# Softmax weights left undivided through the products with v, with one over the sum multiplied in at the silu gate

## The chip, the cores and the metric

The kernel runs on one core of a Trainium2 chip. TensorE (PE) does the matmuls and the transposes, VectorE (DVE) and GpSimd (POOL) the elementwise work, ScalarE (ACT) the activations, and SyncE (SP) issues the DMA transfers from one queue in order. The metric is device microseconds of one execution. Before the change the median of 3 runs is 1141.21 us (1140.96 to 1142.23).

## The reference

One encoder layer with two gated attention branches runs in float32 on a prompt of 512 tokens and a sample of 1024, with shared weights:

```python
h = rmsnorm(x, norm_g)
qa, ka, va, za, qb, kb, vb, zb, ga, gb = split(h @ w_in)
# branch A: 8 heads, 8 x 16 neighbourhood on a grid; branch B: 8 heads on 2 kv heads, window 128, one sink logit per head
s = q @ k.T / 8 + bias
p = softmax(s)                 # in branch B over [s, sink], the sink's own weight dropped
oa = (p @ va) * silu(za) @ w_o_a
ob = (p @ vb) * silu(zb) @ w_o_b
y = x + (sigmoid(ga) * oa + sigmoid(gb) * ob) @ w_out
```

The softmax's division stands ahead of the product with v; as one over the sum is the same for all keys of a query, it may as well stand behind it.

## The kernel before, in words

Every float32 operand is kept as two halves, a rounded one (names ending in hi, hh, fh) and the remainder (lo, hl, fl), and a product is three matmuls: rounded by rounded, rounded by remainder, remainder by rounded (L761 for the projections, L1286 to L1288 for the dense products). The program does the prompt first and then the sample, each in two phases.

The **attention phase** walks six groups of heads, A0 to A3 with two heads each and B0 and B1 with four. A group loads its weights `w` (L600), has them split by ACT (L602) and DVE or POOL (L607), projects 128 tokens at a time (L761), normalises q and k (DVE L785, POOL L792 and L799, DVE L816), and transposes them on PE (L861). `attend` (L908) computes a block's scores (PE L934). `weigh` (L958) then adds the bias on DVE while keeping the running extreme `mx` (L969), and takes the exponential on ACT with its sum `sm` as a by-product (L978). For branch B it adds the sink to the sum by three small operations (POOL L994, ACT L997, POOL L999). It takes one over the sum (DVE L1002), multiplies each 128 x 256 or 128 x 384 tile of weights `sb` by it (DVE L1010 or POOL L1008), transposes the weights on PE (L1026), splits them (ACT L1032, DVE L1037), multiplies by v on PE (L1063), and stores the outputs to `o_d` in DRAM.

The **dense phase** first computes the gate inputs z, chunk by chunk (c = 0 to 7, 128 channels each, 512 tokens at a time). `post_z` (L1406) takes the silu on ACT (L1395), loads the attention outputs back as `ot` (L1417), for chunks 4 to 7 adds two of them, and multiplies them into the gate (helper `tt`, L1162, on DVE or POOL). Its result is needed only when the merge products start, after the gates g. Weight tiles `raw` are loaded (L1250), split (L1168, L1173) and used by PE, in part by Strassen's scheme. Some gate products, called fills, are pulled ahead into the attention phase (`fill_gates`, L1474, its raw weights in two `fr` buffers, bank `d`).

What sets the order: the operations are recorded with a priority, engines they may run on and a planned time, and a list scheduler (`Flow.run`, L207) replays them against those planned times; an operation goes into an engine's queue when it is planned to be ready, the lowest priority number first. The queues so written are fixed and each engine works its own in order. So an edit of one operation can move all others. The planner multiplies planned times of ACT, DVE and POOL by `SLACK` 1.1 in the attention phase.

The z products beyond the first two wait for `exps_done` (L1133), which follows all exponentials, since the silu needs another table on ACT.

Of the kernel before, what the change touches and what calls it, by code (L numbers as in the profile page):

```python
# [40 lines left out]
P = 128  # L41
# [313 lines left out]
def encoder_kernel(  # L355
# [45 lines left out]
        rpb_x[geo.nt] = dpool.tile([8, P, 3 * geo.cw * 16], F32, tag=f"rpb_x{geo.nt}", name=f"rpb_x{geo.nt}")  # L401
    r_d = dpool.tile([NT_S // P, P], F32, tag="r_d", name="r_d")
    t_d = dpool.tile([4, 4, P, NT_S // 2], F32, tag="t_d", name="t_d")
    o_d = {geo.nt: dpool.tile([2, 8, P, geo.nt], F32, tag=f"o_d{geo.nt}", name=f"o_d{geo.nt}") for geo in (gp, gs)}

    def expand(geo, h, lo):
# [24 lines left out]
    def bank(tag):  # L431
        return f.value(pspool, [P, 512], F32, tag, BANKS[tag])
# [215 lines left out]
    def attention_phase(geo, hh, hl, h_ops, mask_d, early, late):  # L648

        nb, nt = geo.nb, geo.nt  # L650
        kt = f.value(early, [P, 4, nt], F32R, "kt", 1)
        stores = {(c, n): [] for c in range(8) for n in range(nt // 512)}
        exps = []

        def tile_(shape, dt, tag, bufs):
            return f.value(early if tag in ("sq", "ss", "rs_v", "rs_r", "v", "q", "qt", "qk") else late, shape, dt, tag, bufs)
# [248 lines left out]
            )  # L905
            return q, [a, b]

        def attend(br, gi, g, batch, nb_t, info, prio):  # L908

            nh = 2 if br == "A" else 4  # L910
            k0 = 2 * (gi % 2)
            states = []
            for block in batch:
                sums = tuple(tile_([P, 4], F32, tag, 3) for tag in ("mx", "sm", "rs", "es"))
                pss = [bank("x") for _ in range(nh)]
                sbs = [tile_([P, GW], F32, "sb", 8 if nt == NT_S else 9) for _ in range(nh)]
                states.append((block, sums, pss, sbs))

            def places(block):
                runs, tiles, _ = block  # L920
                return runs, tiles, len(tiles) * P, tiles[1] - tiles[0], br == "A" and shifted

            def emit(e):

                for block, _, pss, _ in states:
# [18 lines left out]
            o = f.op(  # L944
                (("pe", ns),), emit, prio, new=[v for _, _, pss, sbs in states for v in (*pss, *sbs)],
                use=[queries(block) for block in batch], after=[o for b in batch for t in b[1] for o in info[t][2]],
                hold=[kt],
            )
            for block, _, _, sbs in states:
                for sb in sbs:  # L950
                    sb.writers.clear()
                for s in (k0, k0 + 1):
                    for t in block[1]:
                        reads.setdefault((s, t), []).append(o)
            for state in states:
                weigh(br, gi, g, *state, nb_t, info, prio)

        def weigh(br, gi, g, block, sums, pss, sbs, nb_t, info, prio):  # L958

            nh = 2 if br == "A" else 4  # L960
            runs, tiles, table = block
            nw = len(tiles)
            width = nw * P
            mx, sm, rs, es = sums

            def score(i, ps, sb):
                def emit(e, i=i, ps=ps, sb=sb):
                    init = 3.0e38 if br == "A" else nsink[:, 4 * g + i : 4 * g + i + 1]
                    dve.tensor_tensor_reduce(  # L969
                        out=sb.t[:, :width], in0=ps.t[:, :width], in1=bias_of(br, nb_t, i, table), scale=1.0,  # L970
                        scalar=init, op0=ALU.add, op1=ALU.min, accum_out=mx.t[:, i : i + 1],
                    )

                kw = {"new": [mx], "into": [sb]} if i == 0 else {"into": [mx, sb]}
                d = f.op((("dve", DVE_(width) + 60),), emit, prio, use=[ps, nb_t, sink_v], **kw)

                def emit(e, i=i, sb=sb):
                    act.activation(  # L978
                        sb.t[:, :width], sb.t[:, :width], AF.Exp, bias=mx.t[:, i : i + 1], scale=-1.0,
                        accum_out=sm.t[:, i : i + 1],  # L980
                    )

                kw = {"new": [sm], "into": [sb]} if i == 0 else {"into": [sm, sb]}
                x = f.op((("act", ACT_(width) + 182),), emit, prio, use=[sb], after=[d], **kw)
                exps.append(x)
                mx.left += 1
                x.vals = [*x.vals, mx]

            for i, (ps, sb) in enumerate(zip(pss, sbs)):
                score(i, ps, sb)  # L990
            if br == "B":
                f.op(
                    (("pool", 160),),
                    lambda e: nc.gpsimd.tensor_tensor(es.t, mx.t, nsink[:, 4 * g : 4 * g + 4], op=ALU.subtract),  # L994
                    prio, new=[es], use=[mx],
                )
                f.op((("act", 100),), lambda e: act.activation(es.t, es.t, AF.Exp), prio, use=[es], into=[es])  # L997
                f.op(
                    (("pool", 160),), lambda e: nc.gpsimd.tensor_tensor(sm.t, sm.t, es.t, op=ALU.add),  # L999
                    prio, use=[es, sm], into=[sm],  # L1000
                )
            f.op((("dve", 90),), lambda e: dve.reciprocal(rs.t[:, :nh], sm.t[:, :nh]), prio, new=[rs], use=[sm])  # L1002
            for i in range(nh):

                def emit(e, i=i):
                    sb = sbs[i].t[:, :width]
                    if e == "pool":
                        nc.gpsimd.tensor_tensor(sb, sb, rs.t[:, i : i + 1].to_broadcast([P, width]), op=ALU.mult)  # L1008
                    else:
                        dve.tensor_scalar(sb, sb, rs.t[:, i : i + 1], None, op0=ALU.mult)  # L1010

                f.op(
                    (("dve", 68 + 0.68 * width), ("pool", 30 + 2 * width)), emit, prio,
                    use=[rs, sbs[i]], into=[sbs[i]],
                )
            blocks = [(c, i) for c in range(nw) for i in range(nh)]
            pts = []
            for b in range(0, len(blocks), 4):
# [75 lines left out]
            else:  # L1094
                for e in range(2):
# [6 lines left out]
                    for c in (4 + 2 * g, 5 + 2 * g):  # L1102
                        for n in range(nt // 512):
                            stores[c, n].append(o)

        f.slack = SLACK
        groups = [("A", 0), ("A", 1), ("A", 2), ("A", 3), ("B", 0), ("B", 1)]
        for gi, (br, g) in enumerate(groups):
# [10 lines left out]
                for i in range(4)  # L1119
            ]  # L1120
            nb_t = tables(br, g, lead - 1)
            info, waiting = {}, []
            for t in range(nb):
                prio = lead + t
                v, qk = project(br, w, t, prio)
                info[t] = (v, *make_qk(br, gi, t, qk, prio))
                waiting += [b for b in (a_blocks if br == "A" else b_blocks) if max(b[1]) == t]
                size = 2 if br == "A" else 1
                while len(waiting) >= size:
                    batch, waiting = waiting[:size], waiting[size:]  # L1130
                    attend(br, gi, g, batch, nb_t, info, prio - (bool(waiting) or t < nb - 1))
        f.slack = 1
        exps_done = f.op((("act", 0),), lambda e: None, prio, after=exps)  # L1133
        return stores, exps_done, exps[-40]

    def dense_phase(geo, hh, hl, h_ops, o_stores, exps_done, start, opened, tp, up, p0, p1, p2, x_t, y_t, classic, fill, after_gates=None, side=None):
# [269 lines left out]
        def post_z(c, a, n, v, in_psum, prio):  # L1406
# [13 lines left out]
            ot, ov, sv = ots[0], lambda: ots[0].t[:, :n], lambda: sg.t[:, :n]  # L1420
            if len(ots) > 1:
                tt(ov, ov, lambda: ots[1].t[:, :n], ALU.add, n, prio, use=ots, into=[ot])
            if c < 4:
# [363 lines left out]
```

## Time and profile before

| | |
|---|---|
| median of 3 runs | 1141.21 us |
| profiled execution: its time, its span | 1145.24 us, 1143.4 us |
| PE busy | 1129.6 us of the span, 6115 matmuls |
| DVE, ACT, POOL busy | 858.3, 645.1, 319.4 us |
| granted PE clock, mean | 0.998 |
| prompt attention, prompt dense, sample attention, sample dense | about 0 to 214, 214 to 397, 397 to 788, 788 to 1143 us |

The span runs from the first to the last instruction; what is outside it in the profiled execution is 1.84 us. A row of a group gives line, engine, operation, tiles, shape and count, then busy us, mean ns of one, and the idle time of the engine just before with what ended it. Matmul durations overlap: the time PE needs for one is seen from one start to the next.

### The profile page before, as it was taken

The numbers are of one execution on the slowest core, as the hardware profiler recorded it, in microseconds if no ns is written. First come the engines' busy times: TensorE is split into PE (matmuls) and PEld (weight loads), VectorE is DVE, ScalarE is ACT, GpSimd is POOL, SyncE is SP. The second block draws the span as 40 slices with busy tenths as digits, with TensorE's granted clock in tenths as the row PEclk, the third lists the DMA queues.
The fourth block names the chain that finished last, engine by engine and source line by source line (L and its number), as shares of the span: only waits on it lengthen the run. The fifth ranks groups of instructions, "written<-read, shape, count | busy, mean of one in ns | idle before, by whom it ended". The sixth has DMA issues, their size and how long they took to land.

```text
span 1143.4 us, 18577 instructions
## 1 busy us (share of the span) xinstructions
PE 1129.6 (99%) x6115; PEld 981.9 (86%) x6115; DVE 858.3 (75%) x1994; ACT 645.1 (56%) x1477; POOL 319.4 (28%) x420
## 2 busy tenths in 40 slices
PE   8999999999999999999999999999999999999998
PEld 7989988888888889999899988888888888788887
DVE  6868797587766467887868888886878665497984
ACT  6767997544433246574659888875633334342320
POOL 4644443000010044443514343420123221032110
PEclk9999999999999999999999999999999999999999
DMA  7844643488797422121313214135767545564072
GB/s 267 275 140 129 189 118 97 106 257 256 237 277 210 157 91 72 29 79 29 91 31 93 72 38 121 46 111 160 262 179 228 194 161 186 196 230 130 28 221 93
DMA packets 129314, 168.26 MB, mean 147 GB/s; under 512 B 28809, under 2 KB 67473, under 8 KB 129218
## 3 DMA queue, kind: packets, MB, share of 16 engines
q1 hardware_dynamic: 129218, 167.08, 47.9%
q8 instruction: 48, 0.79, 0.3%
q14 instruction: 48, 0.39, 0.1%
HBM read 128.22 MB, written 43.54 MB: 150 GB/s over the span
## 4 chain that ended last, share of the span: by engine, by line
PE 92%; DMA 3%; DVE 2%; ACT 1%; POOL 1%; issue 1%; SPq 0%; POOLq 0%; DVEq 0%; ACTq 0%
PE p L761 23%; PE x L1288 10%; PE x L1287 10%; PE x L1286 10%; PE x L1063 5%; PE x L1026 5%; PE x L934 5%; PE p L1287 4%; PE p L1286 4%; PE p L1288 4%; PE d L1286 4%; PE d L1288 4%; PE d L1287 4%; PE x L861 2%; DMA w<-in_w_att_dram 1%
## 5 line engine op out<-in xcount | busy, mean ns | idle before, releaser
L761 PE MATMUL p<-whi,hh 128*128 128x384 f32 x384 | 133.8, 349 | 0.0
L761 PE MATMUL p<-whi,hl 128*128 128x384 f32 x384 | 132.7, 345 | 0.0
L761 PE MATMUL p<-wlo,hh 128*128 128x384 f32 x384 | 132.3, 345 | 0.0
L978 ACT ACTIVATE sb<-sb,mx 128x384 f32<-128x384 f32 (+1 forms) x192 | 107.8, 566 | 24.1 <-DVE mx L969 23.7
L761 PE MATMUL p<-whi,hb 128*128 128x384 f32 x384 | 107.8, 346 | 0.0
L1168 ACT ACTIVATE whi<-raw 128x512 fp32r<-128x512 f32 (+1 forms) x124 | 73.8, 607 | 60.2 <-PE x L1287 29.5
L1287 PE MATMUL x<-T,whi 128*128 128x512 f32 x256 | 99.7, 390 | 0.2 <-DVE T L1173 0.2
L1286 PE MATMUL x<-T,whi 128*128 128x512 f32 x256 | 99.7, 389 | 0.0
L1288 PE MATMUL x<-T,wlo 128*128 128x512 f32 x256 | 99.6, 389 | 0.0
L1037 DVE TENSOR_TENSOR pp<-x,pp 128x512 fp32r<-128x512 f32 (+1 forms) x136 | 82.6, 638 | 20.8 <-ACT pp L1032 19.7
L1288 PE MATMUL x<-hh,wlo 128*128 128x512 f32 (+1 forms) x232 | 89.8, 387 | 0.0
L1287 PE MATMUL x<-hl,whi 128*128 128x512 f32 (+1 forms) x232 | 89.8, 387 | 0.0
L1286 PE MATMUL x<-hh,whi 128*128 128x512 f32 (+1 forms) x232 | 89.8, 387 | 0.0
L1173 POOL TENSOR_TENSOR wlo<-raw,whi 128x512 fp32r<-128x512 f32 (+1 forms) x27 | 35.6, 1323 | 182.7 <-ACT whi L1168 182.6
L1173 DVE TENSOR_TENSOR wlo<-raw,whi 128x512 fp32r<-128x512 f32 (+1 forms) x97 | 65.3, 680 | 25.8 <-ACT whi L1168 25.4
L1032 ACT ACTIVATE pp<-x 128x512 fp32r<-128x512 f32 (+1 forms) x136 | 71.0, 560 | 24.0 <-PE x L1026 22.8
L799 POOL TENSOR_TENSOR rs_r<-rs_v,mhalf 128x4 f32<-128x4 f32 (+1 forms) x72 | 79.6, 1106 | 5.7
L792 POOL TENSOR_SCALAR rs_v<-ss 128x4 f32<-128x4 f32 (+1 forms) x72 | 26.8, 373 | 182.3 <-DVE ss L785 179.6
L1063 PE MATMUL x<-pp,v 128*128 128x256 f32 (+1 forms) x368 | 76.7, 322 | 0.0
L761 PEld LDWEIGHTS p<-whi,hl 128*128 128x128 f32 x384 | 73.1, 190 | 1.3 <-issue 1.0
L761 PEld LDWEIGHTS p<-whi,hh 128*128 128x128 f32 x384 | 73.1, 190 | 1.1 <-issue 0.5
L761 PEld LDWEIGHTS p<-wlo,hh 128*128 128x128 f32 x384 | 73.0, 190 | 0.9 <-issue 0.5
(351 smaller groups left out, 3012.9 us busy)
## 6 DMA issues: line engine op xcount, KB each, us to landing
raw<-in_w_g_dram SPq DMA_DIRECT2D x84, 256.0 KB
w<-in_w_att_dram SPq DMA_DIRECT2D x46, 384.0 KB
ot<-o_d SPq DMA_DIRECT2D x36, 256.0 KB
g_d<-C SPq DMA_DIRECT2D x34, 256.0 KB
raw<-in_w_z_dram SPq DMA_DIRECT2D x32, 256.0 KB
raw<-in_w_out_dram SPq DMA_DIRECT2D x32, 256.0 KB
fr<-in_w_g_dram SPq DMA_DIRECT2D x28, 256.0 KB
C<-g_d SPq DMA_DIRECT2D x24, 256.0 KB
```

Source lines behind the costliest of these rows:

```text
L761: pe.matmul(ps.t[:, :GW], part[u](k), mv.t[:, c], start=k == 0 and m == 0, stop=k == KC - 1 and m == 2,)
L799: lambda e: nc.gpsimd.tensor_tensor(r.t[:, :nn], rv.t[:, :nn], mhalf[:, :nn], op=ALU.pow),
L934: pe.matmul(pss[2 * pair + i].t[:, :width], q.t[rows, u, at : at + P], kv[:, tiles[0] : tiles[-1] + 1 : step], start=n == 0, stop=n == 2,)
L978: act.activation(sb.t[:, :width], sb.t[:, :width], AF.Exp, bias=mx.t[:, i : i + 1], scale=-1.0, accum_out=sm.t[:, i : i + 1],)
L1032: lambda e, pt=pt, pp=pp, nn=nn: act.activation(pp.t[:, 0, :nn], pt.t[:, :nn], AF.Copy),
L1037: lambda e, pt=pt, pp=pp, nn=nn: dve.tensor_tensor(pp.t[:, 1, :nn], pt.t[:, :nn], pp.t[:, 0, :nn].bitcast(F32), op=ALU.subtract),
L1063: pe.matmul(out(), v.t[:, vs], mv(), start=first, stop=last)
L1168: (("act", ACT_(n)),), lambda e: act.activation(hi(), src(), AF.Copy), prio,
L1173: lambda e: engines[e].tensor_tensor(lo(), src(), hi().bitcast(F32), op=ALU.subtract), prio,
L1286: pe.matmul(out, hi.t[:, cs], mh(), start=first and k == 0, stop=False, **more)
L1287: pe.matmul(out, hi.t[:, cs], ml(), start=False, stop=False, **more)
L1288: pe.matmul(out, lo.t[:, cs], mh(), start=False, stop=last and k == len(ws) - 1, **more)
```

## The change

The multiplication of the weights by one over the sum is taken out of `weigh`, with the reciprocal and the three sink operations of each block. `mx` and `sm` are now one tile each per group, with a column for each head and block. After a group's last block a new function `norms` does the sink operations and the reciprocal once on the whole tile, transposes it on PE, copies it on ACT and stores it to a DRAM tensor `n_d` (one row per head). `post_z` loads the two heads' rows of its chunk, each spread over 64 partitions, into an `fr` buffer `rn`, and multiplies `ot` by it before the gate. `exps_done` also waits for the sink exponentials of `norms`.

```diff
@@ attention_phase, weigh
-            mx, sm, rs, es = sums
+            mx, sm = sums
+            col = lambda i: slice(i * nb + c0, i * nb + c0 + 1)
+            c0 = (a_blocks if br == "A" else b_blocks).index(block)
...
-            if br == "B":
-                f.op(
-                    (("pool", 160),),
-                    lambda e: nc.gpsimd.tensor_tensor(es.t, mx.t, nsink[:, 4 * g : 4 * g + 4], op=ALU.subtract),
-                    prio, new=[es], use=[mx],
-                )
-                f.op((("act", 100),), lambda e: act.activation(es.t, es.t, AF.Exp), prio, use=[es], into=[es])
-                f.op(
-                    (("pool", 160),), lambda e: nc.gpsimd.tensor_tensor(sm.t, sm.t, es.t, op=ALU.add),
-                    prio, use=[es, sm], into=[sm],
-                )
-            f.op((("dve", 90),), lambda e: dve.reciprocal(rs.t[:, :nh], sm.t[:, :nh]), prio, new=[rs], use=[sm])
-            for i in range(nh):
...
-                    if e == "pool":
-                        nc.gpsimd.tensor_tensor(sb, sb, rs.t[:, i : i + 1].to_broadcast([P, width]), op=ALU.mult)
-                    else:
-                        dve.tensor_scalar(sb, sb, rs.t[:, i : i + 1], None, op0=ALU.mult)
...
+        def norms(br, g, mx, sm, prio):
+
+            nh, h0 = (2, 2 * g) if br == "A" else (4, 8 + 4 * g)
+            w = nh * nb
+            if br == "B":
...
+                f.op((("pool", 350),), emit, prio, use=[mx, sm], into=[mx])
+                ends.append(f.op((("act", 150),), lambda e: act.activation(mx.t[:, :w], mx.t[:, :w], AF.Exp), prio, use=[mx], into=[mx]))
+                f.op(
+                    (("pool", 350),), lambda e: nc.gpsimd.tensor_tensor(sm.t[:, :w], sm.t[:, :w], mx.t[:, :w], op=ALU.add),
+                    prio, use=[mx, sm], into=[sm],
+                )
+            f.op((("dve", 160),), lambda e: dve.reciprocal(sm.t[:, :w], sm.t[:, :w]), prio, use=[sm], into=[sm])
+            ps, st = bank("x"), tile_([32, P], F32, "norms", 1)
+            f.op((("pe", 120),), lambda e: pe.transpose(ps.t[:w, :P], sm.t[:, :w], ident), prio, new=[ps], use=[sm])
+            f.op(
+                (("act", ACT_(P, False)),), lambda e: act.activation(st.t[:w], ps.t[:w, :P], AF.Copy), prio, new=[st], use=[ps]
+            )
+            dst = n_d[nt][h0 : h0 + nh].rearrange("h (b n) -> (h b) n", n=P)
+            o = sp(lambda: nc.sync.dma_start(dst, st.t[:w]), 512 * w, prio, use=[st])
+            for c in range(h0 // 2, (h0 + nh) // 2):
+                stores[c, "norm"].append(o)
...
+            norms(br, g, *sums, prio + 1)
         f.slack = 1
-        exps_done = f.op((("act", 0),), lambda e: None, prio, after=exps)
+        exps_done = f.op((("act", 0),), lambda e: None, prio, after=[*exps, *ends])
@@ dense_phase, post_z
+            rn = f.value(wpool, [P, nh], F32, "fr", 2)
+            runs = [(0, a // nb, m)]
+            if c < 4:
+                off = 64 if geo.cw == 16 else 0
+                runs = [(0, (a - off) % nt, n)] if a >= off else [(0, nt - off, off), (off, 0, n - off)]
+            parts = [(j, r) for j in range(2) for r in runs]
+            for j, (d0, s0, w) in parts:
...
+                    src = n_d[nt][2 * c + j : 2 * c + j + 1, :]
+                    nc.sync.dma_start(dst, bass.AP(tensor=src.tensor, offset=src.offset + s0, ap=ap))
...
+                dma(emit, 256 * w, prio - 0.5, after=o_stores[c, "norm"], **kw)
+            tt(ov, ov, lambda: rn.t[:, :n], ALU.mult, n, prio, use=[ot, rn], into=[ot])
             if c < 4:
                 tt(sv, sv, ov, ALU.mult, n, prio, use=[sg, ot], into=[sg])
```

The change also moves instructions, since the planner places everything anew. Three places are shown that the prediction speaks of.

ACT in the prompt's attention phase, near 68 us of the profile, where two weight splits (`whi`) stand ahead of a block's exponentials (`sb,sm<-sb,mx`); `sq`, `v`, `kt` and `qt` belong to the projection of the next tokens, `junk` is the sample's norm, `pp` the split of transposed weights. Before:

```order
L780 ACTIVATE sq<-p 128x256
L806 ACTIVATE v<-p 128x2x64
L602 ACTIVATE whi<-w_940 128x768
L602 ACTIVATE whi<-w_957 128x768
L978 ACTIVATE sb,sm<-sb,mx 128x256 x4
L780 ACTIVATE sq<-p 128x256
L806 ACTIVATE v<-p 128x2x64
L460 ACTIVATE junk,ns<-xt 128x1024
L1032 ACTIVATE pp<-x 128x512
```

The same place after:

```order
L1174 ACTIVATE fh<-fr 128x512
L603 ACTIVATE whi<-w_931 128x768
L603 ACTIVATE whi<-w_942 128x768
L461 ACTIVATE junk,ns<-xt 128x1024
L980 ACTIVATE sb,sm<-sb,mx 128x256
L883 ACTIVATE kt<-x,gcol 128x128
L897 ACTIVATE qt<-x,gq 128x128
L980 ACTIVATE sb,sm<-sb,mx 128x256 x3
L1007 ACTIVATE pp<-x 128x512
```

The two weight splits still stand ahead of the exponentials, and the norm `junk` and a pair of q and k copies now stand there too.

PE in the prompt's attention phase, after the change, at the end of group A1 (`x<-ident,sb` transposes weights, `x<-pp,v` is the product with v, L762 the projection, `x<-ident,sm` the new transpose of `norms`):

```order
L862 MATMUL x<-ident,qk 128x128 x2
L762 MATMUL p<-whi,hh 128x384
L1001 MATMUL x<-ident,sb 128x128 x4
L1038 MATMUL x<-pp,v 128x256 x4
L762 MATMUL p<-wlo,hh 128x384
L762 MATMUL p<-whi,hl 128x384
L1001 MATMUL x<-ident,sb 128x128 x4
L1100 MATMUL x<-ident,sm 8x128
L762 MATMUL p<-whi,hh 128x384
```

The new transpose stands right behind the four transposes of the group's last weights.

SP in the sample's dense phase, after the change, where chunks 3 to 5 of z are gated (`fr<-n_d` the new reads, `ot<-o_d` the attention outputs, `raw` the weights of z and g, `u_d<-C` the stores of the gated result):

```order
L1443 DMA fr<-n_d_80 64x8x64 x2
L1256 DMA raw<-in_w_z_dram 128x512 x2
L1423 DMA ot<-o_d_82 128x512
L1408 DMA u_d_95<-C 128x512 x2
L1423 DMA ot<-o_d_82 128x8x64
L1443 DMA fr<-n_d_80 64x8x64
L1408 DMA u_d_95<-C 128x512
L1423 DMA ot<-o_d_82 128x8x64
L1256 DMA raw<-in_w_g_dram 128x512
L1443 DMA fr<-n_d_80 64x8x64
```

The new reads stand between the weight loads on the one queue.

More of the change, by code (lines that the diff above doesn't have):

```diff
@@ L403, in encoder_kernel @@
     t_d = dpool.tile([4, 4, P, NT_S // 2], F32, tag="t_d", name="t_d")
+    n_d = {geo.nt: dpool.tile([16, geo.nt], F32, tag=f"n_d{geo.nt}", name=f"n_d{geo.nt}") for geo in (gp, gs)}
     o_d = {geo.nt: dpool.tile([2, 8, P, geo.nt], F32, tag=f"o_d{geo.nt}", name=f"o_d{geo.nt}") for geo in (gp, gs)}
@@ L651, in attention_phase @@
         kt = f.value(early, [P, 4, nt], F32R, "kt", 1)
-        stores = {(c, n): [] for c in range(8) for n in range(nt // 512)}
+        stores = {(c, n): [] for c in range(8) for n in (*range(nt // 512), "norm")}
         exps = []
@@ L913, in attend @@
             for block in batch:
-                sums = tuple(tile_([P, 4], F32, tag, 3) for tag in ("mx", "sm", "rs", "es"))
                 pss = [bank("x") for _ in range(nh)]
                 sbs = [tile_([P, GW], F32, "sb", 8 if nt == NT_S else 9) for _ in range(nh)]
-                states.append((block, sums, pss, sbs))
+                states.append((block, pss, sbs))
             def places(block):
@@ L923, in emit @@
             def emit(e):
-                for block, _, pss, _ in states:
+                for block, pss, _ in states:
                     runs, tiles, width, step, whole = places(block)
@@ L944, in attend @@
             o = f.op(
-                (("pe", ns),), emit, prio, new=[v for _, _, pss, sbs in states for v in (*pss, *sbs)],
+                (("pe", ns),), emit, prio, new=[v for _, pss, sbs in states for v in (*pss, *sbs)],
                 use=[queries(block) for block in batch], after=[o for b in batch for t in b[1] for o in info[t][2]],
@@ L948, in attend @@
             )
-            for block, _, _, sbs in states:
+            for block, _, sbs in states:
                 for sb in sbs:
@@ L970, in emit @@
                         out=sb.t[:, :width], in0=ps.t[:, :width], in1=bias_of(br, nb_t, i, table), scale=1.0,
-                        scalar=init, op0=ALU.add, op1=ALU.min, accum_out=mx.t[:, i : i + 1],
+                        scalar=init, op0=ALU.add, op1=ALU.min, accum_out=mx.t[:, col(i)],
                     )
-                kw = {"new": [mx], "into": [sb]} if i == 0 else {"into": [mx, sb]}
+                kw = {"into": [mx, sb]} if mx.writers else {"new": [mx], "into": [sb]}
                 d = f.op((("dve", DVE_(width) + 60),), emit, prio, use=[ps, nb_t, sink_v], **kw)
@@ L1121, in attention_phase @@
             nb_t = tables(br, g, lead - 1)
+            sums = [tile_([P, 32], F32, tag, 2) for tag in ("mx", "sm")]
             info, waiting = {}, []
```

35 lines of the change are left out of this document (19 added, 16 removed).

## The prediction

> **What bounds the kernel now.** I read the page's busy shares first, then the chain of waits, then who waits for whom on PE.
>
> ```profile
> span 1143.4 us, 18577 instructions
> PE 1129.6 (99%) x6115; PEld 981.9 (86%) x6115; DVE 858.3 (75%) x1994; ACT 645.1 (56%) x1477; POOL 319.4 (28%) x420
> ...
> PE 92%; DMA 3%; DVE 2%; ACT 1%; POOL 1%; issue 1%; SPq 0%; POOLq 0%; DVEq 0%; ACTq 0%
> ```
>
> PE is idle for 13.8 us in all, and 92% of the chain that ended last is its own work. A busy PE need not be a full one, so the pace has to be looked at: one projection matmul starts 0.17 us after the last, a dense one 0.23 us, here and in the stretches without attention alike.
>
> ```profile
> 482.00 0.33 PE L761 MATMUL p<-whi,hh 128*128 128x384 f32 x1
> 482.18 0.33 PE L761 MATMUL p<-wlo,hh 128*128 128x384 f32 x1
> ...
> 776.59 1.47 PE L1026 MATMUL x<-ident,sb 128*128 128x128 f32 x12
> 777.82 0.48 PE L1286 MATMUL d<-hh,fh 128*128 128x512 f32 x1
> 778.14 0.40 PE L1287 MATMUL d<-hl,fh 128*128 128x512 f32 x1
> 778.37 0.40 PE L1288 MATMUL d<-hh,fl 128*128 128x512 f32 x1
> ```
>
> So what is left to win is what PE waits for, and that view is short (waited for, us in total, times, longest):
>
> ```profile
> PE x L1644 <- DMA rb<-in_norm_row_dram: 4.6, 1, 4.6
> PE x L861 <- DVE qk L816: 3.1, 5, 1.0
> PE x L1026 <- DVE sb L1010: 2.3, 2, 2.0
> ```
>
> Of these 10.0 us, 4.6 are the start. Only the 2.3 us of the third row name the multiplication that is taken out, and 2.0 of them are one place. There the clock row has more to say than the wait (each stretch: PE, PEld, DVE, ACT, POOL busy, granted clock, DMA share, GB/s):
>
> ```profile
> 70.00:72.00 2.00, 0.86 (x5) 0.73 (x5) 1.43 (x6) 2.00 (x8) 1.40 (x2) 0.86 0.12 11
> 72.00:74.00 2.00, 2.00 (x9) 1.91 (x8) 1.56 (x6) 1.98 (x6) 1.76 (x5) 0.50 0.85 293
> 74.00:76.00 2.00, 2.00 (x13) 2.00 (x12) 1.18 (x3) 0.60 (x1) 2.00 (x3) 0.79 0.06 24
> ```
>
> After the idle 2 us the clock is granted by half for a while: 2 x 0.14, 2 x 0.50 and 2 x 0.21 us, 1.7 us of clock in all. With the wait, this place costs 3.7 us. The Trainium skill's page "TensorE: Matmul & The Clock Gate" (Part 1: The HAM clock gate) has the clock fall to half only after about 3.4 us of idleness; here 1.96 us were followed by it, so the row and not the rule decides. By the rule the 1.7 us would not hang on this wait, and the sum below, which leaves them where they are, would be the same.
>
> **The change part by part.** What leaves and comes on the engines beside PE, from the groups (busy us, mean ns, idle before):
>
> ```profile
> L1010 DVE TENSOR_SCALAR sb<-sb,rs 128x384 f32<-128x384 f32 (+1 forms) x141 | 51.9, 415 | 1.1
> L1008 POOL TENSOR_TENSOR sb<-sb,rs 128x384 f32<-128x384 f32 (+1 forms) x51 | 36.6, 735 | 39.3 <-DVE rs L1002 38.0 <-PE d L1288 1.2
> L1002 DVE RECIPROCAL rs<-sm 128x2 f32<-128x2 f32 (+1 forms) x72 | 12.0, 166 | 18.9 <-ACT sb L978 10.7 <-POOL sm L999 7.2
> L1162 DVE TENSOR_TENSOR ot<-ot 128x512 f32<-128x512 f32 x11 | 7.6, 689 | 9.5 <-DMA ot<-o_d 8.5 <-issue 1.0
> ```
>
> In the attention phases DVE loses 51.9 us of multiplications and 10 of its 12.0 us of reciprocals (60 of 72 go), POOL 36.6 us. In the dense phases 24 products `ot` by `rn` come, 8 for the prompt and 16 for the sample, at the 0.69 us of the last row 16.6 us, and 56 reads of 128 KB or less, 6.3 MB. The balance is good for DVE and POOL, and PE waits for neither: the multiplications lay beside PE's work except in the 2.3 us. So this is costed at nothing; the cover is PE's own queue, which runs through.
>
> *PE's new work.* Twelve transposes of `norms`. Twelve transposes take 1.23 us in the row at 776.59, and the matmul behind them starts its successor 0.32 us later instead of 0.23, 1.32 us for 12 or 0.11 each. All on the path: **+1.3 us**. Nothing on PE is removed.
>
> *The wait of these transposes.* In the second order above, the transpose of `sm` stands right behind the four of the last weights, and it needs, past the last exponential, the reciprocal on DVE. The trace has that piece of chain, since so far all transposes stood behind it:
>
> ```profile
> 423.74 0.50 ACT L978 ACTIVATE sb<-sb,mx 128x256 f32<-128x256 f32 x1
> ...
> 424.36 0.17 DVE L1002 RECIPROCAL rs<-sm 128x2 f32<-128x2 f32 x1 [1.68 <-ACT sb L978]
> ...
> 424.98 0.81 PE L1026 MATMUL x<-ident,sb 128*128 128x128 f32 x4 [0.30 <-DVE sb L1010]
> ```
>
> From the exponential's start to its reader, the reciprocal, it is 0.62 us, and from there to PE with the multiplication 0.62 more. The four transposes ahead take 0.44, by the 0.11 each, and need no reciprocal. So at most 0.2 us is bare each time while DVE is free, 2.4 us for twelve; at least nothing. The nearest row, the wait of 2.3 us in 72 blocks behind the same chain, gives 12 x 2.3 / 72 = 0.4 us: **+0.4 us** (0 to 2.4). Behind PE there wait the projection and, through it, everything; behind the reciprocal on DVE the splits of weights.
>
> *The place at 71 us.* What PE waited for there was not the multiplication alone:
>
> ```profile
> 61.69 6.46 DMA w<-in_w_att_dram
> ...
> 68.18 0.85 ACT L602 ACTIVATE whi<-w 128x768 fp32r<-128x768 f32 x1 [3.59 <-DMA w<-in_w_att_dram]
> 68.93 0.49 ACT L978 ACTIVATE sb<-sb,mx 128x256 f32<-128x256 f32 x1
> ...
> 71.14 1.17 PE L1026 MATMUL x<-ident,sb 128*128 128x128 f32 x4 [1.96 <-DVE sb L1010]
> ...
> 71.32 1.05 ACT L460 ACTIVATE junk<-xt 128x1024 bf16<-128x1024 f32 x1
> 72.84 0.36 ACT L882 ACTIVATE kt<-x,gcol 128x128 fp32r<-128x128 f32 x1
> 73.09 0.37 ACT L896 ACTIVATE qt<-x,gq 128x128 fp32r<-128x128 f32 x1
> ```
>
> A weight transfer took 6.46 us, ACT's split of it stood at the head of ACT's queue, and the exponentials behind it began at 68.93. In the order after the change the two splits stand there still, and behind them `junk`, one exponential, `kt`, `qt` and the second exponential that the transposes need. By these rows: 68.93, plus 1.04 for `junk`, 0.49, twice 0.25 for the copies, and the 0.62 from an exponential's start to its reader, 71.6 us for PE's start. PE comes there later too: counted by starts, 1.3 us more of matmuls stand ahead of these transposes, so its idle time begins at 69.2 + 1.3 = 70.5 and is 1.1 us in place of 1.96: **-0.8 us**. Whether the half clock goes with it is open: 1.96 us had it, the longest `qk` wait of 1.0 us did not. Bounds: -3.7 if the weights land a little earlier, +2 if the norm's input `xt`, queued on SP behind them, lands that much later and holds the exponentials. I leave the 1.7 us where they are.
>
> *The other wait of this kind*, 2.3 less 1.96, goes: **-0.3 us**. The `qk` waits (3.1 us) hang on the squares on ACT, DVE L785, POOL and DVE L816, none of which is edited; an emptier POOL and DVE may shorten them, another order may lengthen them, by half each way: 0 (-1.5 to +1.5).
>
> *The dense phases.* The new products and reads fall into these stretches:
>
> ```profile
> 240.00:280.00 40.00, 40.00 (x179) 33.10 (x178) 37.08 (x71) 20.50 (x37) 0.00 (x0) 1.00 0.80 246
> 840.00:880.00 40.00, 40.00 (x178) 33.14 (x177) 32.38 (x44) 14.38 (x28) 13.56 (x11) 1.00 0.73 204
> 860.00:870.00 10.00, 10.00 (x46) 8.29 (x45) 9.85 (x13) 4.83 (x10) 7.27 (x5) 1.00 0.64 171
> ```
>
> PE is full in all of them though DVE reaches 37.08 of 40, so its supply of split weights has slack at such loads. The sample's 16 products are 11 us in some 90, which takes DVE from 32.38 of 40, 81%, to about 93%, near the 93% of the first row. The reads of 128 KB on 64 partitions add 4.2 MB (32 by 128 KB) to about 20 MB (90 us by the some 220 GB/s of these rows). What is late next is the gated z, wanted only by the merge products: 0 (0 to +3).
>
> **The sum.** +1.3 + 0.4 - 0.8 - 0.3 = +0.6 us on the profiled span of 1143.4, so 1144.0, and with the 1.84 us outside the span 1145.8 against 1145.24 of that execution. The median of the runs shown is 1141.21; with the same 0.6 it is **1141.8 us**. What a measurement can tell from no change is about 0.2%, 2.3 us, so this is no change.
>
> **The rivals.** *The chains get short and PE's waits go* (faster). In its favour: counted over all transposes, they stood 7.9 us of PE's work behind their scores and now stand 5.0, because the planner no longer allows for reciprocal and multiplication; and the place at 71 us needs less than 1 us to stay at full clock. Against: it needs the weight transfer to keep out of the way. Price: +1.3 - 3.7 - 0.3 - 1.5 = -4.2, 1137.0 us.
>
> *ACT becomes the link that is late* (slower). With 2.9 us less of matmuls between scores and transposes, a hold-up in ACT's queue reaches PE sooner, and the weight splits do hold it up:
>
> ```profile
> ACT whi L602 <- DMA w<-in_w_att_dram: 10.1, 6, 3.6
> ```
>
> 5.5 of these 10.1 us are at 63 and 68 us, 4.6 elsewhere without harm so far. If half of the 4.6 comes through, and the place at 71 us gets 1 us worse: 1.3 + 2.3 + 1.0 = +4.6, 1145.8 us. It decides from the point where PE is idle at one place after `ACT sb` for about 2 us, as the clock then falls too.
>
> *The reads choke the sample's dense phase* (slower). The Trainium skill's page "DMA: Bandwidth & Descriptors" (Specifications) asks for transfers of at least 512 bytes; the sample's 16 reads for chunks 4 to 7 come in rows of 256 bytes, as the `ot` reads there do already. By rows: 2.1 MB at 171/0.64 = 267 GB/s are 7.9 us of all engines, and 840 to 880 us has 0.27 x 40 = 10.8 us free. They fit; if they cost double, as the page's rule lets one fear, 5 us are lacking, weights behind them on SP come late, and half of it reaching PE makes 1141.8 + 2.5 = 1144.3 us. The `ot` reads of the same pattern have not stopped PE, so this is unlikely.
>
> *That the change saves nothing on DVE and POOL* can be left out: 192 multiplications go and 24 products come. It only is not what PE waits for.
>
> **Chances.** Forecast, no change: 0.46; short chains: 0.30; late ACT: 0.17; choked reads: 0.07. So faster 0.30, within 0.2% 0.46, slower 0.24. The forecast's own range is 1138.9 to 1143.5. The range that takes in the first rival's 1137.0 and the second's 1145.8 is 1137.0 to 1146.0.
>
> **What would show it.** In the profile after: twelve transposes of `sm` on PE with idle time of under 0.2 us before each; DVE busy about 45 us less, POOL about 40; PE still 99%, with waits `x<-ident,sb` now on `ACT sb` and in all under 2 us; a single stretch of half clock near 71 us or none; no PE wait between 788 and 900 us. I am wrong on the fast side if there is no half clock after the start, and on the slow side if a PE wait on `ACT sb` is over 2 us, or if PE idles in the z products.

## The result and the profile after

The changed kernel takes 1154.8 us (median of 4, 1154.23 to 1155.79), the kernel before on the same chip 1141.09 us: a ratio of 1.0119, 95% interval 1.0102 to 1.0137. So it is 13.7 us slower, outside the predicted range of 1137 to 1146 us. The profiled execution took 1154.72 us with a span of 1152.9 us.

The page of the changed kernel, busy shares and chain:

```profile
span 1152.9 us, 18448 instructions
PE 1133.5 (98%) x6127; PEld 981.4 (85%) x6127; DVE 829.1 (72%) x1831; ACT 640.8 (56%) x1468; POOL 258.9 (22%) x316
...
PE 84%; DMA 6%; DVE 4%; ACT 2%; POOL 1%; issue 1%; SPq 1%; ACTq 0%; DVEq 0%; POOLq 0%
```

DVE is busy 29 us less and POOL 60 us less (forecast were about 45 and 40), and PE has 12 instructions more, so the change did what it says. But PE's share of the chain that ended last fell from 92% to 84%: work of other engines is now bare. What PE waits for, in the changed kernel:

```profile
PE x L862 <- DVE qk L817: 3.2, 7, 0.6
PE x L1292 <- ACT hh L1174: 2.9, 1, 2.9
PE d L1292 <- ACT fc L1523: 1.7, 2, 1.4
PE x L1001 <- ACT sb L980: 1.3, 4, 0.7
PE x L1293 <- DVE hl L1179: 0.5, 2, 0.3
PE x L1294 <- DVE wlo L1179: 0.4, 2, 0.2
```

The longest wait is new and lies in the prompt's dense phase, at the start of the output product: `hh` is the rounded half of the merged result there, `C`. Around it (stretches of 2 us, the columns as before):

```profile
360.00:362.00 2.00, 0.17 (x1) 0.00 (x0) 2.00 (x4) 0.00 (x0) 0.00 (x0) 1.00 0.78 266
362.00:364.00 2.00, 0.67 (x2) 0.36 (x3) 1.30 (x3) 1.15 (x2) 0.00 (x0) 0.90 0.81 225
364.00:366.00 2.00, 2.00 (x5) 1.61 (x6) 1.29 (x3) 0.63 (x1) 0.00 (x0) 0.50 0.60 177
366.00:368.00 2.00, 2.00 (x8) 1.54 (x8) 0.38 (x1) 0.00 (x0) 0.00 (x0) 0.75 0.88 275
```

PE idles 2.93 us and then has the half clock: 2 x (0.10 + 0.50 + 0.25) = 1.7 us of clock. One wait costs 4.6 us.

For a comparison by stages I cut each trace at two points of PE's queue, its first instruction and the first projection of the sample. In a second profile of the kernel before (run e4, below) and in the changed kernel the cut lies at:

```profile
395.35 0.33 PE L761 MATMUL p<-whi,hh 128*128 128x384 f32 x1
```

```profile
403.96 0.33 PE L762 MATMUL p<-whi,hh 128*128 128x384 f32 x1
```

With PE's start at 4.6 and 4.7 us and the start of its last instruction at 1137.8 and 1149.1, the prompt takes 390.7 us before and 399.3 after, the sample 742.4 and 745.2. Three quarters of the loss are in the prompt, as far as one profile of each tells.

### The profile page after: what moved, and what is told of

It reads as the page before. It is cut to its first block, busy times and chain, and to the rows that moved or that the text cites. A ratio compares the mean times of both kernels' runs of the same rounds, so it can differ in the third digit from the quotient of the medians.

```text
span 1152.9 us, 18448 instructions
## 1 busy us (share of the span) xinstructions
PE 1133.5 (98%) x6127; PEld 981.4 (85%) x6127; DVE 829.1 (72%) x1831; ACT 640.8 (56%) x1468; POOL 258.9 (22%) x316
## 4 chain that ended last, share of the span: by engine, by line
PE 84%; DMA 6%; DVE 4%; ACT 2%; POOL 1%; issue 1%; SPq 1%; ACTq 0%; DVEq 0%; POOLq 0%
PE p L762 23%; PE x L1294 8%; PE x L1293 8%; PE x L1292 8%; PE x L1001 5%; PE x L1038 5%; PE x L934 4%; PE d L1292 4%; PE d L1294 3%; PE d L1293 3%; PE p L1293 3%; PE p L1292 3%; PE p L1294 3%; PE x L862 2%; DMA t_d<-xt 1%
## 5 line engine op out<-in xcount | busy, mean ns | idle before, releaser
L762 PE MATMUL p<-whi,hh 128*128 128x384 f32 x384 | 133.1, 347 | 0.0
L762 PE MATMUL p<-whi,hl 128*128 128x384 f32 x384 | 131.9, 344 | 0.0
L762 PE MATMUL p<-wlo,hh 128*128 128x384 f32 x384 | 130.9, 341 | 0.0
L762 PE MATMUL p<-whi,hb 128*128 128x384 f32 x384 | 106.7, 345 | 0.0
L800 POOL TENSOR_TENSOR rs_r<-rs_v,mhalf 128x4 f32<-128x4 f32 (+1 forms) x72 | 85.6, 1189 | 5.5
L793 POOL TENSOR_SCALAR rs_v<-ss 128x4 f32<-128x4 f32 (+1 forms) x72 | 22.2, 308 | 282.9 <-DVE ss L786 270.0
L1179 POOL TENSOR_TENSOR wlo<-raw,whi 128x512 fp32r<-128x512 f32 (+1 forms) x23 | 29.9, 1300 | 202.8 <-DMA raw<-in_w_g_dram 119.8
L762 PEld LDWEIGHTS p<-whi,hh 128*128 128x128 f32 x384 | 72.5, 189 | 1.3 <-issue 1.0
L762 PEld LDWEIGHTS p<-wlo,hh 128*128 128x128 f32 x384 | 72.6, 189 | 1.0 <-issue 0.7
L762 PEld LDWEIGHTS p<-whi,hl 128*128 128x128 f32 x384 | 72.5, 189 | 0.8 <-issue 0.5
```

The source lines that it names most:

```text
L762: pe.matmul(ps.t[:, :GW], part[u](k), mv.t[:, c], start=k == 0 and m == 0, stop=k == KC - 1 and m == 2,)
L800: lambda e: nc.gpsimd.tensor_tensor(r.t[:, :nn], rv.t[:, :nn], mhalf[:, :nn], op=ALU.pow),
L1179: lambda e: engines[e].tensor_tensor(lo(), src(), hi().bitcast(F32), op=ALU.subtract), prio,
```

## The experiments

**Parts of the change.** Four kernels ran beside the kernel before (median 1141.53 us of 11).

e1 keeps the changed kernel's order and takes the bytes out of the reads:

```diff
-                    dst, ap = rn.t[rows, d0 : d0 + w], [[0, 64], [1, w]]
-                    if c >= 4:
-                        dst, ap = rn.t[rows, :n].rearrange("p (i n) -> p i n", n=m), [[0, 64], [P, nb], [1, m]]
+                    dst, ap = rn.t[rows, d0 : d0 + 16], [[0, 64], [1, 16]]
...
-            tt(ov, ov, lambda: rn.t[:, :n], ALU.mult, n, prio, use=[ot, rn], into=[ot])
+            tt(ov, ov, lambda: rn.t[:, :1].to_broadcast([P, n]), ALU.mult, n, prio, use=[ot, rn], into=[ot])
```

> The changed kernel with every read of one over the sum cut to 16 columns of 64 partitions (4 KB in place of up to 128 KB); the product takes its first column for all tokens, so one over the sum is right for one token in each and left out for the others. Each engine's instructions stand in the same order as in the changed kernel, and as many reads are issued; only 6.3 MB of transfers are gone. Theory A (the bytes of the reads make weights and gate inputs late in the dense phases): the waits of 4.2 us between 240 and 366 us and the half clock behind them go, and the 1.5 us at 792 us: about 1154.8 - 4.2 - 1.7 - 1.9 = 1147 us or less. Theory B (the new order, or the longer use of the ot buffers, makes them late): 1153 to 1156 us.

e2 deletes the lines of `post_z` from `rn = ...` to the product by it.

> The changed kernel without the reads of one over the sum and without the products by it in the dense phases: the division is left out. The attention phases have all of the change, the transposes and the stores of one over the sum with it; the planner places the rest anew. Theory A or B (the loss is in the dense phases): about 1141 us or, with the waits of the attention phase gone, down to 1137. Theory C (the attention phases lose it, by late exponentials): 1148 us or more.

e3 puts those same lines into the kernel before:

```diff
+            rn = f.value(wpool, [P, nh], F32, "fr", 2)
...
+                    src = x_t[0, 2 * c + j : 2 * c + j + 1, :]
+                    nc.sync.dma_start(dst, bass.AP(tensor=src.tensor, offset=src.offset + s0, ap=ap))
...
+            tt(ov, ov, lambda: rn.t[:, :n], ALU.mult, n, prio, use=[ot, rn], into=[ot])
```

> The kernel before, with the division left where it is, and the dense phases of the change: the same 56 reads into the same two fr buffers and the 24 products, their source being rows of the input x (so the gate is multiplied by a wrong factor). Theory A or B: 1141 plus the 8 to 10 us that the dense products lost, 1149 to 1152 us. Theory C: 1140 to 1143 us.

> The kernel before once more, for a second profile, as the first one's execution took 1145.24 us and the median is 1141.21. If the wait of 1.96 us at 71 us and the half clock behind it are what that execution had more than the others, they are absent here and the time is about 1141 us; if they belong to every execution, they are here too.

| kernel | median us (range) | ratio to before, interval | prompt, us | sample, us |
|---|---|---|---|---|
| before (e4: one execution) | 1142.95 | | 390.7 | 742.4 |
| e2, attention part alone | 1147.98 (1146.2 to 1152.0) | 1.0062 (1.0044 to 1.0080) | 393.3 | 745.2 |
| e1, changed, short reads | 1150.25 (1148.5 to 1151.7) | 1.0072 (1.0049 to 1.0095) | 397.4 | 744.4 |
| changed | 1154.8 (1154.2 to 1155.8) | 1.0119 (1.0102 to 1.0137) | 399.3 | 745.2 |
| e3, dense part alone | 1156.71 (1152.6 to 1160.7) | 1.0129 (1.0095 to 1.0162) | 402.6 | 748.4 |

The stage times are those of one profiled execution each; e3's is its slowest, 1160.70 us. The bytes cost 1154.8 - 1150.25 = 4.5 us, in one and the same order. e1 came out between theories A and B: A wanted 8 us or more, and the wait for `hh` stayed at 2.9 us, with the half clock behind it, so the bytes alone do not make it. e2 came out at the edge of theory C, 6.5 us slower without any product or read, and e3, 15 us slower, as C could not have it and above what A or B had. 6.5 and 15 do not add up to 13.7. The suspect is that the planner writes each of these kernels but e1 anew.

In e4 the place at 71 us has neither wait nor half clock:

```profile
70.00:72.00 2.00, 2.00 (x15) 1.78 (x14) 1.96 (x7) 2.00 (x7) 1.44 (x3) 1.00 0.46 124
72.00:74.00 2.00, 2.00 (x16) 1.86 (x15) 1.39 (x5) 1.94 (x5) 1.76 (x5) 1.00 0.72 274
```

They belonged to the one execution that was profiled first, and go with its being 4 us over the median.

**Orders alone.** Two kernels before and two changed ones, with only the planner's factor altered:

```diff
-SLACK = 1.1
+SLACK = 1.11
```

> The kernel before with the planner's factor on planned times of ACT, DVE and POOL at 1.11 in place of 1.10. No work changes, only the order in which the same instructions are queued. Theory D (the order of before is a well-placed one, and nearly any other, whatever it is made by, costs PE some 5 us of waits): 1145 to 1150 us. Theory E (orders of this planner are within 2 us of each other, and what the changed kernel loses comes from its work): 1139 to 1143 us.

> The same with 1.12, a second draw of the order. Theory D: 1145 to 1150 us; theory E: 1139 to 1143 us.

> The changed kernel with the factor at 1.11. Theory D: it may fall on either side, 1146 to 1156 us, and stands no further from the kernels before of the same factors than the 4 to 5 us that the bytes of the reads cost; theory E: 1153 to 1156 us, like the changed kernel.

> The changed kernel with the factor at 1.12. Theory D: 1146 to 1156 us; theory E: 1153 to 1156 us.

e5 took 1143.03 us (1.0008, 0.9994 to 1.0021), e6 1149.79 (1.0061, 1.0039 to 1.0083), e7 1156.70 (1.0137, 1.0119 to 1.0156), e8 1148.54 (1.0058, 1.0037 to 1.0078). Theory E falls as a rule: the same work in another order lost 7 us in e6, and the changed work gained 6 in e8. But theory D did not hold everywhere either: e5 came out where E had it, and e7 0.7 us above what either had. The changed e8 at 1.12 stands no higher than the e6 before at 1.12. e8 also varies from 1141.76 to 1153.38 us over ten executions of one program.

**The wait for `hh`.** What feeds it, in the changed kernel (`ot<-g_d` reads a stored gate for the merge, ACT L1401 is its sigmoid, DVE `C<-C,ot` the sum of both branches):

```profile
272.48 1.10 DVE L1168 TENSOR_TENSOR C<-C,ot 128x512 f32<-128x512 f32 x1
```

```profile
320.16 0.32 SPq L1603 DMA_DIRECT2D ot<-g_d  x1
```

```profile
353.40 0.33 SPq L1603 DMA_DIRECT2D ot<-g_d  x1
...
356.91 0.63 ACT L1401 ACTIVATE ot<-ot 128x512 f32<-128x512 f32 x1 [2.35 <-DMA ot<-g_d]
...
361.70 0.69 DVE L1168 TENSOR_TENSOR C<-C,ot 128x512 f32<-128x512 f32 x1
362.42 0.63 ACT L1174 ACTIVATE hh<-C 128x512 fp32r<-128x512 f32 x1 [2.80 <-DVE C L1168]
...
363.10 0.49 PE L1292 MATMUL x<-hh,whi 128*128 128x512 f32 x1 [2.93 <-ACT hh L1174]
```

The same events in the kernel before (e4), the last gated z, the first and the last read of a stored gate, its sigmoid, `hh`, and PE's 25th matmul of the output product, the first that needs this `hh`:

```profile
263.20 1.09 DVE L1162 TENSOR_TENSOR C<-C,ot 128x512 f32<-128x512 f32 x1
```

```profile
314.00 0.45 SPq L1578 DMA_DIRECT2D ot<-g_d  x1
```

```profile
346.77 0.33 SPq L1578 DMA_DIRECT2D ot<-g_d  x1
```

```profile
349.64 0.63 ACT L1395 ACTIVATE ot<-ot 128x512 f32<-128x512 f32 x1 [1.72 <-DMA ot<-g_d]
...
355.15 0.63 ACT L1168 ACTIVATE hh<-C 128x512 fp32r<-128x512 f32 x1 [2.71 <-DVE C L1162]
```

```profile
357.25 0.39 PE L1286 MATMUL x<-hh,whi 128*128 128x512 f32 x1
```

PE was full there before, but `hh` ended at 355.78, only 1.5 us ahead of its use. After the change the last gated z is 9.3 us later, the first read of a stored gate 6.2 us, the last one 6.6 us, while the output product on PE begins 2.6 us later (354.34 against 351.79 us). The chain's 6.6 us less PE's 2.6 are more than the 1.5 us of slack. The chain is late, PE is not.

In each kernel the read at 353.40 (346.77) is issued when `C<-C,ot` releases one of two `ot` buffers. So the next guess was that ring, and a third buffer the test, paid for with one of the four `C` buffers. PE's order is unchanged, the queues of the other engines are not:

```diff
-        n_c, n_ot = (4, 2) if short else (5, 2)
+        n_c, n_ot = (3, 3) if short else (5, 2)
```

> The changed kernel with three ot and three C buffers in the prompt's dense phase in place of two and four; PE's instructions stand in the same order as in the changed kernel, and 4663 rows of it are the same. Theory F (in the prompt's merge the next read of a stored gate waits for the release of one of the two ot buffers, and that ring of read, sigmoid, product and sum, late by the reads of the z part, makes PE wait 2.9 us for hh and run at half clock behind it): the wait and the half clock go, 1154.8 - 2.9 - 1.7 = about 1150 us. Theory G (it is a matter of the whole phase being late by DMA and DVE, the buffers don't matter): 1153 to 1156 us.

> The same buffers in the kernel before, PE's order again the same as before. It has no such wait, so by theory F nothing changes, 1140 to 1143 us; slower by 2 us or more if one C buffer less costs something of its own.

> The attention part alone (the division left out, as before without reads and products by one over the sum) with the three ot buffers. Theory F: it loses its wait of 1.4 us for hh at 358 us and comes to about 1145 to 1146 us, the rest being the waits for fc and T after 780 us. Theory G: 1147 to 1149 us.

> The changed kernel with three ot buffers and the reads of one over the sum cut to 16 columns (one over the sum is right for one token in each and left out for the others), in the order of the changed kernel with three ot buffers. If bytes and ring add up: 1154.8 - 4.5 - 4.6 = 1145 to 1146 us. If the bytes' 4.5 us were lost by the same ring: like the changed kernel with three ot buffers alone, within 1.5 us.

e9 took 1155.10 us (1.0118, 1.0087 to 1.0149), e10 1141.89 (0.9997, 0.9983 to 1.0011), e11 1147.93 (1.0052, 1.0036 to 1.0068), e12 1151.37 (1.0079, 1.0060 to 1.0097). Theory F falls. The wait got shorter wherever there was one, but not away (e9):

```profile
363.30 0.50 PE L1292 MATMUL x<-hh,whi 128*128 128x512 f32 x1 [2.33 <-ACT hh L1174]
```

It is 2.33 for 2.93 us, 2.13 in e12, 0.34 for 1.40 in e11, and no median moved by more than its spread. In e9 the ring is not the limit: the sigmoid of the last stored gate starts at 352.02 us, 4.9 us earlier than in the changed kernel, and `hh` still starts at 362.62 against 362.42. From 350.72 us until `hh` starts DVE is idle for only 1.4 us, both times waiting for an earlier `hh`; it works sums of the merge and splits of weights one behind the other. So behind the ring stands DVE's queue. e12 under e9 gives the price of the bytes a second time, with the same order in both: 3.7 us, though the ranges of the two overlap.

**More orders**, to part the work from the draw:

> The kernel before with the planner's factor at 1.07. Theory H (order and work share the loss: orders scatter by some 4 us, the changed work costs 5 to 9 us beside it): 1140 to 1150 us, on the mean of all orders of before about 1145. Theory D (all is order): the same here, but then the changed kernel at 1.07 and 1.13 comes to about the same as this one.

> The changed kernel with the factor at 1.07. Theory H: 1149 to 1157 us, 5 to 9 above the kernel before at the same factor on the mean of all pairs. Theory D: 1141 to 1150 us.

> The kernel before with the factor at 1.13. Both theories: 1140 to 1150 us.

> The changed kernel with the factor at 1.13. Theory H: 1149 to 1157 us. Theory D: 1141 to 1150 us.

> The attention part alone (the division left out) with the factor at 1.11. If its 6.5 us at 1.10 were the draw of the order: 1139 to 1145 us. If the attention part costs by itself: 1146 to 1150 us.

> The same with the factor at 1.12. If the loss at 1.10 was the draw: 1139 to 1147 us, by the kernel before at this factor, 1149.8, rather the upper part. If the attention part costs by itself: 1146 to 1154 us.

Medians; behind each, prompt and sample time of its one profiled execution (for 1.10 before that of e4), in us. They come from several sets of runs; the kernel before, run again beside each set, took 1141.1 to 1142.6 us.

| factor | before | changed | attention part alone |
|---|---|---|---|
| 1.07 | 1150.8 (394.9, 746.2) | 1157.2 (400.2, 743.9) | |
| 1.10 | 1141.5 (390.7, 742.4) | 1154.8 (399.3, 745.2) | 1148.0 (393.3, 745.2) |
| 1.11 | 1143.0 (389.8, 743.2) | 1156.7 (397.8, 748.7) | 1146.4 (391.8, 743.4) |
| 1.12 | 1149.8 (397.7, 743.3) | 1148.5 (397.5, 741.7) | 1141.5 (391.1, 740.5) |
| 1.13 | 1156.0 (398.1, 746.8) | 1155.4 (401.1, 743.7) | |
| mean | 1148.2 (394.2, 744.4) | 1154.5 (399.2, 744.6) | 1145.3 (392.1, 743.0) |
| `hh` wait, us | none, none, none, 2.33, 2.83 | 1.75, 2.93, 2.93, 2.93, 2.33 | 1.40, 1.55, none |

e15 missed its range of 1140 to 1150 us under both theories, by 6 us, and e13 and e14 theirs by 0.8 and 0.2: orders scatter more than I had thought. Three readings.

First, the order of the kernel before at 1.10 is the best of its five, 6.7 us under their mean. An edit that makes the planner write PE's queue anew may be expected to give that up on the average, whatever the edit is; five orders are few to say how much.

Second, beside that the work in the dense phases costs something. Pairs of one factor leave it unsettled: 6.3 us on the mean of five (6.4, 13.3, 13.7, -1.3, -0.6), with a standard error of 3.2 us, so an interval of plus or minus 9 us that contains zero. But the factor does not hold the order; the attention part alters it. Five other pairs of these runs differ in the dense part alone, and in them PE's matmuls, by tile and shape, stand in the same order but for at most six of some 6100 (at 1.12 without exception). The other engines' queues take in the 24 products and 56 reads and shift around them. Without and with the dense part, medians, the loss, what the profiled executions lost in the prompt and in the sample, and PE's wait for `hh`, in us:

| attention part, factor | without | with | loss | prompt, sample | `hh` wait |
|---|---|---|---|---|---|
| before, 1.10 | 1141.5 (before) | 1156.7 (e3) | 15.2 | 11.8, 5.9 | none, 2.92 |
| changed, 1.10 | 1148.0 (e2) | 1154.8 (changed) | 6.8 | 6.0, 0.0 | 1.40, 2.93 |
| changed, 1.10, three `ot` | 1147.9 (e11) | 1155.1 (e9) | 7.2 | 8.6, -0.8 | 0.34, 2.33 |
| changed, 1.11 | 1146.4 (e17) | 1156.7 (e7) | 10.3 | 6.0, 5.3 | 1.55, 2.93 |
| changed, 1.12 | 1141.5 (e18) | 1148.5 (e8) | 7.1 | 6.3, 1.2 | none, 2.93 |

The dense part costs 7 to 15 us in every pair, the profiled executions lost at least 6 of them in the prompt, and the wait for `hh` comes or grows each time. Only e18 and e8 have ranges that overlap. That is theory H, and the bytes, 4.5 and 3.7 us, are half to two thirds of the 6.8 and 7.2 us in their orders. So of the 13.3 us between 1141.5 and 1154.8, 6.8 came with the dense part and 6.5 with the attention part and its order.

Third, the attention part alone stands with the kernel before: 1148.0, 1146.4 and 1141.5 against 1141.5, 1143.0 and 1149.8, means 1145.3 and 1144.8. Its 6.5 us at 1.10, 3.4 at 1.11 and -8.3 at 1.12 look like the draw; e17 alone would have spoken for a cost of its own, and three orders can't rule out a small one. At 1.12 it has hardly a wait left:

```profile
PE x L862 <- DVE qk L817: 2.7, 5, 1.0
PE x L1001 <- ACT sb L980: 0.3, 2, 0.2
```

and gains nothing over the best order before (1.0003, 0.9993 to 1.0012), though the 192 multiplications are gone and only the small work of `norms` has come for them. No kernel of these beats the one before.

## Why the prediction was wrong

*What bounds the kernel* was right: PE does, and no order that saved the multiplications got under 1141 us.

*The multiplications cost PE nothing* was right as far as e18 tells.

*The twelve transposes*, +1.3 us, was right. In the changed kernel the product behind a transpose of `sm` starts only 0.03 us after it:

```profile
213.38 0.27 PE L1100 MATMUL x<-ident,sm 128*16 128x128 f32 x1
213.41 0.48 PE L1292 MATMUL p<-hh,whi 128*128 128x512 f32 x1
213.73 0.39 PE L1293 MATMUL p<-hl,whi 128*128 128x512 f32 x1
```

But that product starts its successor 0.32 us later in place of 0.23. Together it is 0.12 us, near the 0.11 of the prediction; a trace read from the transpose's own start to the next one would show a quarter of the cost. *Their wait*, +0.4, was 0.06 us, at one place.

*The place at 71 us*, -0.8, was worked out from an event that e4 and e10 don't have. Against those, the changed kernel has 0.25 and 0.67 us of new wait for `sb` there, without half clock; the 1.1 us of idle time that I worked out for the changed kernel was near, and is a loss of 0.9 and no gain. What failed there is taking one execution, 4 us over its own median, for the kernel. *The other wait of this kind*, -0.3, did not go: the changed kernel waits 0.18 and 0.16 us at 428 us, against 0.3 us before. *The `qk` waits*, 0 (-1.5 to +1.5), went from 2.0 us in e4 to 3.2.

*The dense phases*, 0 (0 to +3), is the step that decided: with PE's order held the term measured 6.8 us at 1.10 and 7 to 15 in all pairs. I quoted the prompt's own row with DVE at 37.08 of 40 and DMA at 0.80 and read a full PE as slack. A full PE says nothing of how early its operands are: the slack at `hh` was 1.5 us. I costed only the sample's reads, and there PE's time is 745.2 us with the dense part and without it (e2). The prompt's 24 reads and 8 products stand between 193 and 272 us, where the gates' weights, the sample's norm and the gates' stores share the DMA engines, and from 240 to 366 us PE idles 4.2 us and loses 1.7 us of clock. The waits that I had ruled out at 788 to 900 us, and named as a sign of being wrong, came too, 0.33 us just ahead of it and 1.36 us in it: fills that attention no longer holds stand among the z products, and their bank waits for ACT, where splits that had waited 1.21 us for a transfer stand ahead. After the change 1672 of PE's instructions stand behind the sample's last scores, in e4 1626. It goes with this order; e18 has no such wait:

```profile
786.80 0.60 ACT L1523 ACTIVATE fc<-d 128x512 f32<-128x512 f32 x1 [3.97 <-DMA g_d<-fc]
...
791.56 1.26 ACT L1174 ACTIVATE T<-U 128x512 fp32r<-128x512 f32 x2 [1.21 <-DMA U<-t_d]
...
793.25 0.58 ACT L1523 ACTIVATE fc<-d 128x512 f32<-128x512 f32 x1
...
793.87 0.50 PE L1292 MATMUL d<-hh,fh 128*128 128x512 f32 x1 [1.36 <-ACT fc L1523]
```

*The rivals.* The short chains came about, and where the order was kind they gave the kernel before's best time and not 1137. The late ACT cost 1.3 us in all, not 4.6. The choked reads, which I gave 7 in 100, were the nearest: bytes that cost about 4 us. But they were placed in the sample for their short rows, and the price lay mostly with the plain rows of the prompt (e1 against the changed kernel: 1.9 us less in the prompt, 0.8 in the sample, single profiles). What was missing among the rivals is the draw of the order itself: five orders of the same work took 1141.5 to 1156.0 us, and only two of them lie in the 9 us from 1137 to 1146.

What stays open is how the dense part makes the chain late. Where PE's order is held, the last gated z ends 10 to 18 us later with it (263.5 us in e2, 273.6 in the changed kernel), and the awaited `hh` 4.5 to 10 us later (358.6 and 363.1). With the reads cut short, in e1, the z still ends at 272.1 us, and `hh` at 360.8: the bytes are a small part of the first delay and half of the second. The wait for `hh` stays at 2.93 us in e1, as PE gets there earlier too. Whether the rest is the issue of the reads, the products on DVE or their places in the queues, no run parts. The 6.5 us that came with the attention part are open in the same way: the orders at 1.11 and 1.12 speak for the draw, and no run has the attention part in the order of the kernel before.

## What to carry to other kernels

Where a planner writes the queues, an edit is two changes, its work and a new draw of the order; draw a few orders of both kernels before a few microseconds are put down to the work. Where a single cost is to be measured, compare kernels in which the engine that bounds the time has the same order: five orders by factor left the cost at 6 plus or minus 9 us, five pairs with PE's order held had it at 7 to 15, and a transfer cut short in place left every queue as it was. Moving work from engines that are not waited for into a phase whose DMA and chain are nearly full can lose even where eight operations become one. And a full engine is not slack: look at how long before its use each operand was ready.

## What the runs showed of the hardware

The half clock keeps to a grid. In the clock record of every run the full clock lasts, from its first grant to the next fall, a whole number of steps of 3.413 us: 58.03 us in the first profile of the kernel before (17 steps), 351.57 in the changed kernel (103), 252.59 in e16 (74). Each stretch of half clock ahead of the last matmul is one such step, in e3 two. What goes before a fall is idle time of PE inside the step that ends there (by the modelled ends of its matmuls). Over all twenty traces, every step with 1.83 us of idle time or more was followed by half clock, and none with 1.5 us or less. In between two were (1.55 us in e3, 1.71 in e14) and three were not (1.63 in e7, 1.73 in e15, 1.78 at the end of e14), so these runs give no sharper edge.

So one idle time of a given length can cost clock or not. In e17 an idle time of 1.55 us lay across the end of a step, no more than 0.95 us of idleness fell into either, and nothing changed:

```profile
356.99 0.49 PE L1292 MATMUL x<-hh,whi 128*128 128x512 f32 x1 [1.55 <-ACT hh L1174]
```

```profile
358.00:360.00 2.00, 2.00 (x10) 1.62 (x10) 1.55 (x3) 0.64 (x1) 0.00 (x0) 1.00 0.71 212
```

In e15 even 2.04 us, 1.73 in one step and 0.31 in the next, left the clock at full:

```profile
270.26 0.50 PE L1288 MATMUL x<-hh,wlo 128*128 128x512 f32 x1 [2.04 <-DVE wlo L1173]
```

In e14 1.75 us did not; with it PE was idle for 1.71 us of one step:

```profile
363.84 0.50 PE L1292 MATMUL x<-hh,whi 128*128 128x512 f32 x1 [1.75 <-ACT hh L1174]
```

```profile
364.00:366.00 2.00, 1.78 (x7) 1.15 (x8) 1.77 (x4) 0.94 (x2) 0.00 (x0) 0.94 0.54 191
366.00:368.00 2.00, 2.00 (x6) 1.56 (x5) 0.63 (x2) 0.00 (x0) 0.00 (x0) 0.50 0.92 339
368.00:370.00 2.00, 2.00 (x8) 1.59 (x7) 0.00 (x0) 0.49 (x1) 0.00 (x0) 0.71 0.70 168
```

The Trainium skill's page "TensorE: Matmul & The Clock Gate" (Part 1: The HAM clock gate) puts the fall after about 3.4 us of idleness; these traces do not agree: 1.55 us within a step were enough once, and 1.83 us or more always. In this kernel a wait of some 2 us costs 1.7 us of clock on top of itself when it falls into one step, as at 71 us in the first profile, and none when it is cut in two, as in e15.
